# A new order of the steps of four attention layers, given to a list scheduler

## The chip, the cores and the metric

The kernel runs on one core of one Trainium2 chip. The metric is device time in microseconds (us) of one execution, as the median of several runs.

## The reference, cut to what matters

Two blocks follow one another on an input of 256 tokens by 1024 columns, in float32. The first has an attention layer with eight NSA heads and four differential heads ("Even"), an MLP, an attention layer with sixteen MoBA heads ("Odd"), and a second MLP. The second block has two layers of one kind: three branches (a gated delta rule, latent attention and RWKV7) read one projection; their outputs are joined, multiplied by a gate, and projected out.

```python
for i in range(DEPTH):                      # first block, DEPTH = 2
    hn = rms_norm(x, norm_mix[i])
    mix = even_mixer(hn, ...) if i % 2 == 0 else odd_mixer(hn, ...)
    x = x + mix
    x = x + sqrelu_mlp(rms_norm(x, norm_mlp[i]), mlp_w1[i], mlp_w2[i])

# even_mixer: projections, NSA and differential attention, out projection
return jnp.concatenate([o_a, o_b], axis=-1) @ w_out

# second block, gated delta rule: chunks of 64 rows, a state carried along
def step(s, inp):
    w_c, u0_c, p_c, qg_c, kd_c, ge_c = inp
    u = u0_c - jnp.einsum('nhcd,nhde->nhce', w_c, s)
    o = jnp.einsum('nhcd,nhde->nhce', qg_c, s) + jnp.einsum('nhij,nhje->nhie', p_c, u)
    s = ge_c[..., None, None] * s + jnp.einsum('nhcd,nhce->nhde', kd_c, u)
    return s, o
```

RWKV7 is a second recurrence with a carried state, which the kernel also computes in chunks. Both recurrences run forward and backward over the tokens.

## The kernel before, in words

Every layer keeps the 256 tokens as two tiles of 128 rows in SBUF. A weight matrix comes in slabs: `wload` (line 692) issues DMAs into a tile named `wt`, lets ScalarE cast the slab to a rounded copy and VectorE subtract that copy, which leaves a high and a low part in tiles named `fr`. `mm3` (line 719) multiplies each pair as three TensorE products, high by high and the two mixed ones. So in the profile a matmul `ps<-fr 128x256` or `ps<-fr 128x512` is one product of a projection, and a matmul `ps<-sb` belongs to attention, to a transpose or to a recurrence. All other tiles are named `sb` (SBUF) and `ps` (PSUM).

The four attention layers are classes: `Even` (line 1134), `Odd` (1436) and `Second` (1505, used for both layers of the second block). Each consists of parts, and each part is a Python generator that yields after each of its steps:

- Even: `q0`, `q1`, `keys`, `vals`, `gates`, `kc` (projections), `dp0` and `dp1` (projections of two pairs of differential heads), `attn0` to `attn3` (NSA attention), `cmpk` and `comp` (the compressed branch), `diff0` and `diff1` (differential attention), `out_a` and `out_b` (out projection, in two sets of rows of the weight).
- Odd: `proj0` to `proj3`, `attn0` to `attn3`, `out_a`, `out_b`.
- Second: `gdn_proj`, `gdn_prep`, `gdn_inv` (inverses of triangular 64 by 64 matrices, by many small products), `gdn_uw`, `gdn_steps` (the serial recurrence), `gdn_end`; `rwkv_proj`, `rwkv_prep`, `rwkv_inv`, `rwkv_mats`, `rwkv_steps` (the second serial recurrence), `rwkv_end`; `mla_proj`, `mla_attend`, `mla_end`; `gates` (projection and nonlinearity of the output gate), `out_a`, `out_b`.

A string `ORDER` in each class (lines 1140, 1441 and 1576; `Second` has one for each of its layers) says how many steps of which part come next. `Layer.weave` (line 1065) reads it; a word such as `rwkv_inv*4` runs four steps of that part, and the dictionary `NEEDS` says which parts must have ended before a part may begin:

```python
for word in order.split():
    n, _, steps = word.partition("*")
    if n not in parts:
        assert ended >= set(self.NEEDS.get(n, "").split()), (n, ended)
        ...
    for _ in range(int(steps or 1)):
        if self.step(parts[n]):
            ended.add(n)
```

A step does not issue instructions. It notes them (`Order.note`, line 269), and after the last layer `Order.flush` (line 385) hands the whole program to a list scheduler, `Order.plan` (line 412). That walks over the noted operations with a window of 600; on each engine it takes, among the operations whose inputs it believes ready, the one noted first, with a bias for some; it places tiles in SBUF and PSUM as it goes, and does so for several ways of packing, of which one is kept. `put` (line 613, its call is line 614) then issues each operation, so every instruction in the trace carries line 614. Each engine executes its own list in order. The `ORDER` strings thus set priorities, and through them the order of PE (TensorE matmul), DVE (VectorE), ACT (ScalarE), POOL (GpSimd) and SP, whose queue issues the weight loads.

The out projection of a layer has two parts. `out_most` (line 1100), called by `out_a`, multiplies six row slabs of the weight into PSUM; `out_rest` (line 1116), called by `out_b`, multiplies the two others. Their products have 512 columns.

Of the kernel before, what the change touches and what calls it, by code (L numbers as in the profile page):

```python
# [1133 lines left out]
class Even(Layer):  # L1134
# [3 lines left out]
             "attn3": "q1 keys vals gates bias", "diff0": "dp0 lam bias", "diff1": "dp1 lam bias", "cmpk": "kc",  # L1138
             "comp": "cmpk q0 q1 attn0 attn1 attn2 attn3", "out_a": "comp diff0", "out_b": "diff1"}
    ORDER = (  # L1140
# [5 lines left out]

    def run(self):
        net = self.net
# [287 lines left out]
class Odd(Layer):  # L1436
# [2 lines left out]
    NEEDS = {"attn0": "proj0", "attn1": "proj1", "attn2": "proj2", "attn3": "proj3", "out_a": "attn0 attn1 attn2",  # L1439
             "out_b": "attn3"}  # L1440
    ORDER = (
# [4 lines left out]

    def run(self):
        net = self.net
# [56 lines left out]
class Second(Layer):  # L1505
# [41 lines left out]
    def start(self):  # L1547
# [26 lines left out]
        self.ts(self.rh, r, 0.5)  # L1574

    ORDER = (
        "gdn_proj*10 rwkv_proj gdn_proj*4 rwkv_proj gdn_proj*2 rwkv_proj*2 gdn_prep*3 rwkv_proj gdn_prep*3 rwkv_proj "
        "gdn_inv*2 rwkv_proj gdn_inv*2 rwkv_proj gdn_inv rwkv_proj*3 gdn_inv*6 rwkv_proj*2 gdn_inv*2 rwkv_proj "
        "gdn_inv*6 rwkv_proj gdn_inv*2 rwkv_proj gdn_inv rwkv_proj gdn_inv*3 rwkv_proj gdn_inv*5 rwkv_prep gdn_inv*3 "
        "rwkv_prep gdn_inv*6 rwkv_prep*4 gdn_inv gdn_uw rwkv_prep gdn_uw*3 rwkv_prep*2 gdn_uw*2 rwkv_inv*2 gdn_uw "  # L1580
        "rwkv_inv gdn_uw rwkv_inv*4 gdn_uw rwkv_inv gdn_uw rwkv_inv*11 gdn_uw rwkv_inv*2 gdn_steps rwkv_inv gdn_steps "
        "rwkv_inv gdn_steps*2 rwkv_inv*2 gdn_steps rwkv_inv gdn_steps gates gdn_steps*2 rwkv_mats gdn_steps rwkv_inv "
        "rwkv_mats rwkv_inv rwkv_mats rwkv_inv gates rwkv_inv*2 rwkv_mats rwkv_inv*2 rwkv_mats gates*2 rwkv_mats "
        "gdn_steps gates rwkv_mats*2 rwkv_inv gates rwkv_inv gdn_steps rwkv_mats gates rwkv_inv gates rwkv_inv gates "
        "rwkv_mats rwkv_inv rwkv_mats rwkv_steps*2 mla_proj rwkv_steps gates rwkv_steps mla_proj rwkv_steps*2 "
        "mla_proj rwkv_steps mla_proj rwkv_steps*2 gates*2 rwkv_steps mla_proj*3 rwkv_steps mla_proj*2 rwkv_steps "
        "mla_proj gdn_end rwkv_end mla_proj mla_attend*6 rwkv_end mla_attend*6 gdn_end*2 mla_attend*4 rwkv_end*2 "
        "out_b mla_end out_b mla_end out_a out_b out_a*9",
        "gdn_proj*16 gdn_prep*2 gates gdn_prep gates*2 gdn_prep*2 gates gdn_prep gdn_inv gates rwkv_proj gdn_inv*2 "
        "rwkv_proj gdn_inv*3 rwkv_proj gdn_inv*2 rwkv_proj*4 gdn_inv rwkv_proj gdn_inv rwkv_proj gdn_inv*10 "  # L1590
        "rwkv_proj*5 gdn_inv rwkv_proj*3 gdn_inv rwkv_proj gdn_inv*17 rwkv_prep gdn_inv rwkv_prep*4 gdn_uw rwkv_prep "
        "gdn_uw rwkv_prep gdn_uw rwkv_prep gdn_uw rwkv_prep gdn_uw*2 rwkv_inv gdn_uw*3 rwkv_inv*2 gdn_uw*2 gdn_steps "
        "rwkv_inv*2 gdn_steps rwkv_inv*5 gates rwkv_inv*4 gdn_steps rwkv_inv gates rwkv_inv gates rwkv_inv*3 "
        "gdn_steps*3 gates rwkv_inv gdn_steps rwkv_inv gdn_steps gates*3 rwkv_inv rwkv_mats gdn_steps*2 rwkv_mats "
        "rwkv_inv rwkv_mats*3 rwkv_inv rwkv_mats rwkv_inv*8 gdn_steps rwkv_inv rwkv_mats gdn_end mla_proj rwkv_inv "
        "rwkv_mats*3 mla_proj rwkv_inv*4 gdn_end mla_proj rwkv_mats mla_proj*4 rwkv_steps*2 mla_proj rwkv_steps "
        "mla_proj*2 gdn_end rwkv_steps mla_proj rwkv_steps mla_attend*6 rwkv_steps*2 mla_attend*7 rwkv_steps "
        "mla_attend*2 rwkv_steps*2 mla_attend mla_end rwkv_steps mla_end rwkv_steps out_a*2 rwkv_end*2 out_a*3 "
        "rwkv_end out_a*3 rwkv_end out_b*3 out_a*2")

    def run(self):
        net, l = self.net, self.l
# [1012 lines left out]
```

## Time and profile before

| what | us |
|---|---|
| median of 3 runs | 1231.8 (1231.16 to 1233.77) |
| profiled execution, its own time | 1228.06 |
| its span | 1226.3 |
| PE busy | 1073.2 (88%) |
| PEld busy (weight loads of TensorE) | 950.9 (78%) |
| DVE busy | 832.9 (68%) |
| ACT busy | 577.1 (47%) |
| POOL busy | 75.7 (6%) |

The profiled execution is one execution of the program, 3.7 us under the median. The mean granted clock of TensorE over it was 0.905 of 2.4 GHz. The stages follow one another: Even to about 158 us, the first MLP to about 341, Odd to about 461, the second MLP to about 643, the second block's layers to about 928 and 1215, then the final norm and the output. The busy share is an average over these stages, and they have different limits: in the MLPs PE has hardly a gap, while in the second block PE, DVE and ACT take turns in waiting for each other. All idle times are therefore read stage by stage.

### The profile page before, as it was taken

Reading aid. Unit: us, or ns where it says so; the run is one execution under the profiler, and the core shown is the slowest. Engines: PE = TensorE matmul, PEld = TensorE weight load, DVE = VectorE, ACT = ScalarE, POOL = GpSimd, SP = SyncE. Lnnn points to the kernel's source line nnn. Section 1 sums busy time; section 2 is a strip of 40 time slices with the busy share of each in tenths; the row PEclk is TensorE's granted clock in tenths of the full one; section 3 lists DMA queues with packets and bytes.
Section 4 is the critical chain, followed back from the end, with each engine's and each line's share of the span. In section 5 each row is a group of like instructions: output and inputs, shape, how many; then the busy total and the mean of one; then the engine's idle time right before and its main releaser. Section 6 shows DMA issues by size and latency. Waiting matters only on the chain. (4 is left out here: it accounts for less than half of the span.)

```text
span 1226.3 us, 22320 instructions
## 1 busy us (share of the span) xinstructions
PE 1073.2 (88%) x8969; PEld 950.9 (78%) x8969; DVE 832.9 (68%) x1757; ACT 577.1 (47%) x1069; POOL 75.7 (6%) x150
## 2 busy tenths in 40 slices
PE   8999899999998999999997974489899895768895
PEld 7887699999897979999986873478568784657663
DVE  5556775545565566555488899962877889788445
ACT  4565454444436555444354543226564453332751
POOL 0000000000000000000001310002200310001200
PEclk9999899999998999999998885699899797678797
DMA  9930375565542454675671410142214342102110
GB/s 265 275 106 21 118 222 174 177 200 195 174 148 82 143 172 139 222 224 174 210 247 36 132 44 1 51 117 84 70 41 127 86 117 73 36 13 90 51 50 35
DMA packets 129682, 151.51 MB, mean 124 GB/s; under 512 B 15979, under 2 KB 111338, under 8 KB 129578
## 3 DMA queue, kind: packets, MB, share of 16 engines
q1 hardware_dynamic: 128745, 147.89, 38.7%
q0 software_dynamic: 832, 2.20, 0.7%
q8 instruction: 70, 1.15, 0.4%
q14 instruction: 35, 0.28, 0.1%
HBM read 147.42 MB, written 1.07 MB: 121 GB/s over the span
## 5 line engine op out<-in xcount | busy, mean ns | idle before, releaser
L614 PE MATMUL ps<-fr 128*128 128x256 f32 (+3 forms) x5112 | 788.1, 315 | 23.2 <-DVE fr L614 9.2
L614 PEld LDWEIGHTS ps<-fr 128*128 128x128 f32 (+1 forms) x5112 | 714.4, 194 | 83.6 <-DVE fr L614 14.4
L614 PE MATMUL ps<-sb 64*64 64x64 f32 (+14 forms) x3857 | 309.3, 286 | 118.3 <-DVE sb L614 83.3
L614 PEld LDWEIGHTS ps<-sb 64*64 64x64 f32 (+5 forms) x3857 | 241.1, 171 | 179.8 <-DVE sb L614 77.3
L614 DVE TENSOR_TENSOR fr<-wt,fr 128x1024 fp32r<-128x1024 f32 (+4 forms) x269 | 314.7, 1202 | 55.4 <-ACT fr L614 54.8
L614 ACT CAST fr<-wt 128x1024 fp32r<-128x1024 f32 (+4 forms) x269 | 263.0, 1022 | 80.7 <-DMA wt<-in_mlp_w 25.6
L614 ACT ACTIVATE sb<-sb 128x256 f32<-128x256 f32 (+8 forms) x347 | 163.3, 504 | 209.4 <-DVE sb L614 187.2
L614 DVE TENSOR_TENSOR sb<-ps,sb 128x256 f32<-128x256 f32 (+7 forms) x169 | 85.8, 517 | 171.5 <-ACT sb L614 90.0
L614 ACT ACTIVATE sb<-ps 128x384 f32<-128x384 f32 (+7 forms) x166 | 77.3, 475 | 228.2 <-PE ps L614 207.3
L614 DVE TENSOR_TENSOR sb<-sb 128x256 f32<-128x256 f32 (+24 forms) x436 | 146.1, 348 | 10.9 <-POOL sb L614 4.2
L614 DVE SCALAR_TENSOR_TENSOR sb<-sb 128x256 f32<-128x256 f32 (+8 forms) x228 | 88.8, 407 | 20.6 <-ACT sb L614 17.0
L614 DVE TENSOR_TENSOR sb<-sb,ps 128x512 f32<-128x512 f32 (+3 forms) x82 | 46.7, 582 | 31.9 <-PE ps L614 31.5
L614 POOL TENSOR_TENSOR sb<-sb 128x384 f32<-128x384 f32 (+4 forms) x55 | 52.8, 980 | 171.3 <-PE ps L614 97.3
L614 ACT ACTIVATE sb<-ps,sb 128x256 f32<-128x256 f32 (+3 forms) x70 | 34.8, 542 | 47.7 <-PE ps L614 45.7
L614 DVE TENSOR_TENSOR fr<-sb,fr 128x512 fp32r<-128x512 f32 (+1 forms) x38 | 24.7, 649 | 21.5 <-ACT fr L614 21.3
L614 ACT CAST fr<-sb 128x512 fp32r<-128x512 f32 x32 | 19.9, 621 | 32.4 <-DVE sb L614 32.4
L614 DVE COPY sb<-ps 128x384 f32<-128x384 f32 (+9 forms) x45 | 21.3, 478 | 19.7 <-PE ps L614 19.2
L614 POOL MEMSET sb<- 128x2 f32 (+3 forms) x59 | 5.7, 140 | 463.6 <-DVE sb L614 286.8
L614 DVE TENSOR_SCALAR sb<-sb 128x2 f32<-128x2 f32 (+15 forms) x119 | 26.2, 234 | 4.8 <-POOL sb L614 2.0
L614 DVE CUSTOM_DVE_ANT_0 sb<-ps,sb 128x128 f32<-128x128 f32 (+1 forms) x80 | 24.6, 352 | 6.7 <-PE ps L614 3.5
L614 POOL TENSOR_SCALAR sb<-sb 128x2 f32<-128x2 f32 (+1 forms) x8 | 2.5, 312 | 416.9 <-DVE sb L614 416.9
L614 ACT ACTIVATE fr<-ps,sb 128x256 fp32r<-128x256 f32 x52 | 19.8, 488 | 11.5 <-PE ps L614 10.8
(30 smaller groups left out, 162.8 us busy)
## 6 DMA issues: line engine op xcount, KB each, us to landing
wt<-in_mlp_w SPq DMA_DIRECT2D x128, 512.0 KB
wt<-in_w_in SPq DMA_DIRECT2D x38, 512.0 KB
wt<-in_od_w_in SPq DMA_DIRECT2D x24, 512.0 KB
wt<-in_w_out SPq DMA_DIRECT2D x16, 512.0 KB
wt<-in_ev_w_in SPq DMA_DIRECT2D x14, 512.0 KB
wt<-in_ev_w_in SPq DMA_DIRECT2D x16, 256.0 KB
wt<-in_ev_w_out SPq DMA_DIRECT2D x8, 512.0 KB
wt<-in_od_w_out SPq DMA_DIRECT2D x8, 512.0 KB
```

What stands on the lines that cost most here:

```text
L614: fn(*a, **k)
```

## The change

The four `ORDER` strings are replaced: that of Even, that of Odd, and the two of Second. The parts, their steps, the operations in them, `NEEDS`, the scheduler and the tiles are as they were. The strings are tables; two pieces show their form, the end of Even's and the end of that of the last layer:

```diff
@@ Even @@
-        "diff1*2 attn3 diff1 attn1 diff1 cmpk dp0 cmpk attn3 cmpk*2 dp0 cmpk comp dp0 out_b dp0 diff0 comp diff0*4 "
-        "out_b diff0*4 out_b diff0 comp out_a*10")
+        "attn1 diff1 cmpk*2 diff0 cmpk attn3 attn2 attn3 diff1 diff0 comp diff0*6 comp diff0 comp diff0 out_a out_b "
+        "out_a*3 out_b*2 out_a*6")
...
@@ Second, its second layer @@
-        "mla_attend*2 rwkv_steps*2 mla_attend mla_end rwkv_steps mla_end rwkv_steps out_a*2 rwkv_end*2 out_a*3 "
-        "rwkv_end out_a*3 rwkv_end out_b*3 out_a*2")
+        "rwkv_steps*3 mla_attend*2 rwkv_end mla_attend*3 mla_end*2 rwkv_end out_a*3 rwkv_end out_a*3 rwkv_end out_b "
+        "out_a out_b*2 out_a*3")
```

Three places of PE's list follow. A row is a run of equal matmuls; `ps<-fr 128x512` is a product of the out projection.

**End of Even, PE, before.** The `128x128` rows are transposes of the attention outputs, the `128x256` rows multiply their probabilities by values, and the 24 products `128x512` are `out_b`'s.

```order
L614 MATMUL ps<-sb 128x128 x2
L614 MATMUL ps<-sb 128x256 x2
L614 MATMUL ps<-sb 128x128 x9
L614 MATMUL ps<-sb 128x256 x4
L614 MATMUL ps<-sb 128x128 x3
L614 MATMUL ps<-fr 128x512 x24
L614 MATMUL ps<-sb 128x128 x3
L614 MATMUL ps<-fr 128x512 x4
L614 MATMUL ps<-sb 128x128 x3
L614 MATMUL ps<-fr 128x512 x19
L614 MATMUL ps<-sb 128x128 x4
L614 MATMUL ps<-fr 128x512 x49
```

The same place of the changed kernel; three more runs of `128x512` (of 2, 2 and 4) stand ahead of these rows, with one to three `128x128` between them.

```order
L614 MATMUL ps<-sb 128x128 x3
L614 MATMUL ps<-fr 128x512 x2
L614 MATMUL ps<-sb 128x128
L614 MATMUL ps<-fr 128x512 x2
L614 MATMUL ps<-sb 128x128 x2
L614 MATMUL ps<-fr 128x512 x4
L614 MATMUL ps<-sb 128x128 x5
L614 MATMUL ps<-fr 128x512 x5
L614 MATMUL ps<-sb 128x256 x4
L614 MATMUL ps<-fr 128x512 x3
L614 MATMUL ps<-sb 128x128 x4
L614 MATMUL ps<-fr 128x512 x72
```

The 24 products that stood in one piece behind the attention's last small products now stand in eight pieces between them, and the other 72 in one piece at the end.

**First layer of the second block, PE, before.** The `64x64` rows are `gdn_inv`, `gdn_uw` and `gdn_steps`; the `128x320` rows are the first products of `gates`; `32x32` and `128x2` belong to `gdn_inv` and `rwkv_prep`.

```order
L614 MATMUL ps<-sb 128x128 x8
L614 MATMUL ps<-sb 32x32 x96
L614 MATMUL ps<-sb 64x64 x33
L614 MATMUL ps<-sb 128x2 x4
L614 MATMUL ps<-sb 64x64 x239
L614 MATMUL ps<-sb 128x128 x8
L614 MATMUL ps<-fr 128x320 x24
L614 MATMUL ps<-sb 128x128 x8
L614 MATMUL ps<-sb 64x64 x13
L614 MATMUL ps<-fr 128x320 x24
```

The same place of the changed kernel:

```order
L614 MATMUL ps<-fr 128x320
L614 MATMUL ps<-sb 128x128 x7
L614 MATMUL ps<-sb 32x32 x96
L614 MATMUL ps<-fr 128x320 x6
L614 MATMUL ps<-sb 64x64
L614 MATMUL ps<-fr 128x320 x7
L614 MATMUL ps<-sb 128x2 x4
L614 MATMUL ps<-fr 128x320 x2
L614 MATMUL ps<-sb 64x64 x103
L614 MATMUL ps<-fr 128x320 x8
L614 MATMUL ps<-sb 64x64 x144
L614 MATMUL ps<-fr 128x320 x24
```

The first 24 products of `gates`, which stood behind all the `64x64` rows, now stand in five pieces in front of them and between them.

**End of the last layer, PE, before.** The `64x64` and `64x256` rows are the last pieces of `rwkv_steps`, the `128x128` rows transposes, the `128x512` rows products of `out_a`, the last 24 of them of `out_b`. Five more `128x512` stand ahead of these rows.

```order
L614 MATMUL ps<-sb 128x128 x4
L614 MATMUL ps<-fr 128x512
L614 MATMUL ps<-sb 128x128 x4
L614 MATMUL ps<-sb 64x256
L614 MATMUL ps<-sb 64x64 x8
L614 MATMUL ps<-sb 64x256 x3
L614 MATMUL ps<-sb 64x64 x8
L614 MATMUL ps<-fr 128x512 x30
L614 MATMUL ps<-sb 64x64 x16
L614 MATMUL ps<-fr 128x512 x36
L614 MATMUL ps<-sb 128x128 x4
L614 MATMUL ps<-fr 128x512 x24
```

The same place of the changed kernel; three `128x512`, 16 `64x64` and 2 `128x128` stand ahead of these rows, and 38 more products `128x512` behind the last.

```order
L614 MATMUL ps<-fr 128x512
L614 MATMUL ps<-sb 128x128 x2
L614 MATMUL ps<-fr 128x512 x2
L614 MATMUL ps<-sb 64x64 x8
L614 MATMUL ps<-sb 128x128 x4
L614 MATMUL ps<-sb 64x64 x8
L614 MATMUL ps<-sb 64x256 x4
L614 MATMUL ps<-fr 128x512 x51
L614 MATMUL ps<-sb 128x128
L614 MATMUL ps<-fr 128x512
L614 MATMUL ps<-sb 128x128 x3
```

Ahead of the last piece of `rwkv_steps` stood 36 products of the out projection, and now 6; behind it stood 60, and now 90.

## Rows read from the trace of the kernel before

**Rows 1.** The page: busy time, share of the span, instructions; DMA busy tenths in 40 slices.

```profile
PE 1073.2 (88%) x8969; PEld 950.9 (78%) x8969; DVE 832.9 (68%) x1757; ACT 577.1 (47%) x1069; POOL 75.7 (6%) x150
...
DMA  9930375565542454675671410142214342102110
```

**Rows 2.** Windows: length, busy PE, PEld, DVE, ACT, POOL, then clock, DMA share, GB/s.

```profile
51.70:105.70 54.00, 51.80 (x441) 47.42 (x439) 32.35 (x105) 37.63 (x108) 0.00 (x0) 1.00 0.42 124
105.70:158.40 52.70, 44.88 (x240) 34.82 (x240) 36.73 (x84) 22.83 (x49) 3.45 (x5) 0.84 0.31 99
377.10:393.00 15.90, 12.44 (x86) 9.79 (x85) 11.54 (x41) 14.39 (x45) 0.00 (x0) 0.79 0.31 99
737.80:772.00 34.20, 18.30 (x427) 16.83 (x429) 33.34 (x91) 9.74 (x16) 0.52 (x1) 0.50 0.07 17
799.60:850.00 50.40, 44.85 (x514) 41.79 (x508) 25.44 (x41) 21.23 (x35) 4.62 (x7) 0.97 0.37 99
1043.00:1075.80 32.80, 23.75 (x436) 22.00 (x431) 23.61 (x47) 11.36 (x18) 0.52 (x1) 0.66 0.15 33
1075.80:1127.00 51.20, 38.14 (x652) 34.97 (x654) 43.11 (x99) 12.17 (x22) 3.13 (x4) 0.83 0.16 53
1127.00:1184.00 57.00, 50.11 (x470) 35.23 (x465) 29.22 (x85) 40.87 (x97) 11.51 (x16) 0.79 0.19 62
```

**Rows 3.** Timeline of PE, end of the last layer: start, us, operation [idle before <-releaser].

```profile
1183.10 7.12 PE L614 MATMUL ps<-fr 128*128 128x512 f32 x30
1190.14 0.68 PE L614 MATMUL ps<-sb 64*64 64x64 f32 x16
1191.30 1.08 PE L614 MATMUL ps<-sb 128*64 128x64 f32 x16 [0.48 <-ACT sb L614]
...
1194.30 8.37 PE L614 MATMUL ps<-fr 128*128 128x512 f32 x34 [0.34 <-DVE fr L614]
1204.60 0.88 PE L614 MATMUL ps<-sb 128*128 128x128 f32 x4 [1.94 <-DVE sb L614]
1206.17 8.57 PE L614 MATMUL ps<-fr 128*128 128x512 f32 x24 [0.69 <-ACT fr L614]
```

**Rows 4.** Timeline of DVE, the same stretch.

```profile
1186.85 0.69 DVE L614 TENSOR_TENSOR sb<-sb,ps 128x512 f32<-128x512 f32 x1 [2.71 <-PE ps L614]
...
1192.42 0.69 DVE L614 COPY sb<-ps 128x512 f32<-128x512 f32 x1 [1.49 <-PE ps L614]
...
1203.35 1.53 DVE L614 TENSOR_TENSOR sb<-sb 128x512 f32<-128x512 f32 x3
```

**Rows 5.** ACT by shape, 1127 to 1184: count, busy, mean ns, idle before.

```profile
L614 ACT ACTIVATE sb<-ps 64x256 f32<-64x256 f32 x19 | 7.2, 378 | 0.8 <-PE ps L614 0.4
...
L614 ACT ACTIVATE sb<-sb 32x256 f32<-32x256 f32 x12 | 4.6, 409 | 0.2
...
L614 ACT ACTIVATE sb<-sb 64x512 f32<-64x512 f32 x4 | 4.4, 1158 | 8.9 <-PE ps L614 8.9
```

**Rows 6.** Timeline of PE, second block's second layer.

```profile
1060.95 4.64 PE L614 MATMUL ps<-fr 128*128 128x256 f32 x20 [0.20 <-DVE fr L614]
...
1066.23 3.12 PE L614 MATMUL ps<-fr 128*128 128x256 f32 x24
```

**Rows 7.** Timeline of PE, second block's first layer.

```profile
792.02 1.56 PE L614 MATMUL ps<-sb 64*64 64x64 f32 x48 [9.57 <-DVE sb L614]
...
801.66 0.56 PE L614 MATMUL ps<-fr 128*128 128x320 f32 x2
...
806.31 3.59 PE L614 MATMUL ps<-fr 128*128 128x320 f32 x13 [0.65 <-DVE sb L614]
```

**Rows 8.** Timeline of PE, end of Even.

```profile
127.08 1.33 PE L614 MATMUL ps<-sb 128*128 128x128 f32 x5 [3.95 <-DVE sb L614]
...
133.72 5.72 PE L614 MATMUL ps<-fr 128*128 128x512 f32 x24
```

**Rows 9.** Timeline of PE, Odd, first attention.

```profile
383.54 5.37 PE L614 MATMUL ps<-sb 128*128 128x128 f32 x20 [3.43 <-ACT sb L614]
```

More of the change, by code (lines that the diff above doesn't have):

```diff
@@ L1441 @@
     ORDER = (
[4 rows of a table removed]
+        "proj1*6 proj0*6 proj2 proj0*3 proj1 attn0 proj1 proj2 attn0 proj2 proj3*2 proj1 proj2*3 proj3 attn1 proj3*3 "
+        "proj2 attn0*2 attn1*2 attn0*2 proj2*2 attn1*3 attn2*4 proj3*2 attn2 proj3 attn3*3 attn2 attn3 out_a attn3*2 "
+        "out_b*2 out_a*5 out_b out_a*3")
     def run(self):
@@ L1576 @@
     ORDER = (
[L1577 to L1586, printed above, removed]
@@ L1587 @@
-        "mla_proj gdn_end rwkv_end mla_proj mla_attend*6 rwkv_end mla_attend*6 gdn_end*2 mla_attend*4 rwkv_end*2 "
-        "out_b mla_end out_b mla_end out_a out_b out_a*9",
-        "gdn_proj*16 gdn_prep*2 gates gdn_prep gates*2 gdn_prep*2 gates gdn_prep gdn_inv gates rwkv_proj gdn_inv*2 "
-        "rwkv_proj gdn_inv*3 rwkv_proj gdn_inv*2 rwkv_proj*4 gdn_inv rwkv_proj gdn_inv rwkv_proj gdn_inv*10 "
-        "rwkv_proj*5 gdn_inv rwkv_proj*3 gdn_inv rwkv_proj gdn_inv*17 rwkv_prep gdn_inv rwkv_prep*4 gdn_uw rwkv_prep "
@@ L1592 @@
[L1592 to L1596, printed above, removed]
@@ L1597 @@
-        "mla_proj*2 gdn_end rwkv_steps mla_proj rwkv_steps mla_attend*6 rwkv_steps*2 mla_attend*7 rwkv_steps "
-        "mla_attend*2 rwkv_steps*2 mla_attend mla_end rwkv_steps mla_end rwkv_steps out_a*2 rwkv_end*2 out_a*3 "
-        "rwkv_end out_a*3 rwkv_end out_b*3 out_a*2")
+        "gdn_proj*10 rwkv_proj gdn_proj*4 rwkv_proj gdn_proj*2 rwkv_proj gdn_prep rwkv_proj gdn_prep*2 rwkv_proj "
+        "gdn_prep*2 rwkv_proj gdn_prep gdn_inv rwkv_proj*2 gdn_inv rwkv_proj gdn_inv*2 rwkv_proj gdn_inv*2 rwkv_proj "
@@ new lines @@
+        "gdn_inv*3 rwkv_proj gdn_inv*6 rwkv_proj gdn_inv*7 rwkv_proj gdn_inv*5 rwkv_proj*3 gdn_inv*2 rwkv_proj "
+        "gdn_inv rwkv_prep*4 gdn_inv*6 rwkv_prep gdn_inv*2 rwkv_prep gdn_inv*2 rwkv_prep gdn_uw*3 rwkv_prep*2 "
+        "rwkv_inv gdn_uw rwkv_inv*17 gdn_uw*4 rwkv_inv*2 gdn_uw rwkv_inv gdn_uw*2 rwkv_inv gdn_steps*2 rwkv_inv "
+        "gdn_steps rwkv_inv gdn_steps rwkv_inv gdn_steps rwkv_inv gdn_steps gates gdn_steps*2 rwkv_inv rwkv_mats "
+        "gdn_steps gates rwkv_mats rwkv_inv*5 rwkv_mats*2 rwkv_inv gates rwkv_mats*2 gates*2 gdn_steps rwkv_mats*2 "
@@ new lines @@
+        "rwkv_inv gates rwkv_inv gdn_steps rwkv_mats gates rwkv_inv gates rwkv_inv rwkv_mats gates rwkv_inv rwkv_mats "
+        "rwkv_steps mla_proj gates rwkv_steps mla_proj rwkv_steps*2 mla_proj rwkv_steps*2 mla_proj rwkv_steps*2 gates "
+        "rwkv_steps mla_proj rwkv_steps mla_proj*3 rwkv_steps mla_proj*2 gates rwkv_steps gdn_end mla_proj "
+        "mla_attend*2 rwkv_end mla_attend*4 rwkv_end mla_attend*2 rwkv_end mla_attend*4 rwkv_end mla_attend gdn_end*2 "
+        "mla_attend*3 out_b mla_end out_b mla_end out_a*8 out_b out_a*2",
@@ new lines @@
+        "gdn_proj*16 gdn_prep*2 gates gdn_prep gates*2 gdn_prep*2 gates gdn_prep gdn_inv gates rwkv_proj gdn_inv*2 "
+        "rwkv_proj gdn_inv*4 rwkv_proj gdn_inv*3 rwkv_proj gdn_inv*4 rwkv_proj gdn_inv rwkv_proj gdn_inv rwkv_proj*2 "
+        "gdn_inv rwkv_proj gdn_inv rwkv_proj*2 gdn_inv*4 rwkv_proj gdn_inv rwkv_proj*2 gdn_inv*2 rwkv_proj gdn_inv "
+        "rwkv_proj gdn_inv rwkv_proj*2 gdn_inv*7 rwkv_prep gdn_inv rwkv_prep gdn_inv rwkv_prep*2 gdn_inv*4 "
+        "rwkv_prep*5 gdn_uw*6 rwkv_inv gdn_uw*2 rwkv_inv*2 gdn_uw rwkv_inv*2 gdn_uw rwkv_inv*8 gdn_uw gdn_steps gates "
@@ new lines @@
+        "rwkv_inv*3 gdn_steps rwkv_inv*4 gdn_steps gates gdn_steps*2 gates rwkv_inv gates gdn_steps*3 gates rwkv_inv "
+        "gates rwkv_inv rwkv_mats gdn_steps*2 rwkv_inv rwkv_mats*4 gates rwkv_inv*2 gdn_steps rwkv_inv*6 rwkv_mats "
+        "gdn_end rwkv_mats mla_proj rwkv_inv rwkv_mats*3 rwkv_inv mla_proj rwkv_inv*2 gdn_end rwkv_inv mla_proj*6 "
+        "rwkv_mats mla_proj rwkv_inv mla_proj*2 rwkv_steps*2 mla_attend rwkv_steps mla_attend rwkv_steps mla_attend*2 "
+        "rwkv_steps*2 mla_attend*3 rwkv_steps mla_attend rwkv_steps mla_attend*2 gdn_end rwkv_steps mla_attend "
```

10 rows, old and new, of the table ORDER are left out of this document.

## The prediction

> **What bounds the kernel now.** I began with the page. PE is busy for 88% of the span, DVE for 68%, ACT for 47% [rows 1]. No engine is full, so no single busy time gives the answer: the layers must be read stage by stage. The windows came next [rows 2]; there the reader is to see three kinds of stretch. In 51.7–105.7 (Even) PE is busy 51.80 of 54.0 us at clock 1.00: PE bounds it. In 737.8–772.0 DVE is busy 33.34 of 34.2 us and PE 18.30: VectorE bounds it. In 105.7–158.4, 377.1–393.0 and 1043.0–1075.8 no engine is full: PE is busy 44.88 of 52.7, 12.44 of 15.9 and 23.75 of 32.8 us, at a clock of 0.84, 0.79 and 0.66. There a chain of small pieces over PE, DVE and ACT sets the time, and an order that lays independent products into its waits can gain. The timelines then show which products stand ahead of a chain, and which behind it.
>
> No operation changes, so each term is a wait filled or opened. The sum is made against the profiled execution, 1228.06 us, which is 3.7 us below the median of 1231.8; at the end I add the 3.7.
>
> **1. End of the last layer: −6 us.** Before, a run of 30 products of 512 columns, 7.12 us from 1183.10, stands directly ahead of the last piece of `rwkv_steps`, whose 16 products follow at 1190.14 with no wait [rows 3]: their inputs were there, PE held them back. VectorE in turn waits 2.71 us for PE at 1186.85 and copies the last result at 1192.42 [rows 4]. Now those 30 stand behind the steps, so the steps can end 7.12 us earlier, at 1192.38 − 7.1 = 1185.3. Then 90 products follow; at 7.12/30 = 0.237 us each they take 21.4, and four transposes 0.9 [rows 3]: PE ends at 1207.6 instead of 1206.17 + 8.57 = 1214.74, which is −7.1. Late next would be `rwkv_end` on VectorE: from the copy at 1192.42 to 1203.35 + 1.53 it takes 12.5 us [rows 4], and the first 51 of the 90 products, 12.1 us, cover it. ScalarE takes some back: its list now has six more copies 64x256 and six more 32x256 ahead of the first `rwkv_steps` copies, 6 × 0.378 + 6 × 0.409 = 4.7 us, while the two weight casts moved up as well fall into its 8.9 us of waiting [rows 5]. Later in the chain that lead shrinks, so I take 1 us off. Ends: −10, if the waits of 1.94 and 0.69 us at 1204.60 and 1206.17 go too; +7, if the chain's end does not move and the 30 products simply follow it.
>
> **2. Second block's second layer, 44 products of `gates`: −2.** They stand at 1060.95 and 1066.23, 4.64 + 3.12 = 7.76 us [rows 6], ahead of the products that lead into `gdn_steps`. Now they stand behind the second of its steps, directly ahead of the third. What is taken from the chain's front is put into its middle: at 0.13 us each (3.12/24) they cost 5.7 there. The difference is 2. Ends: −7.8, if in the new place they fall into waits (PE is busy only 38.14 of 51.2 us in 1075.8–1127 [rows 2]); +6, if the old place was a wait anyway and the new one is not.
>
> **3. Second block's first layer, 24 products of `gates`: −4.** They run from 801.66 to 806.31 + 3.59 = 809.90, 8.24 us, partly waiting for DVE [rows 7], behind the chain of `gdn_steps`, in a stretch where PE is busy 44.85 of 50.4 us [rows 2]. Now they stand between the products of `gdn_inv` and `gdn_uw`, in 737.8–799.6, where PE waits for DVE, up to 9.57 us at a time [rows 7]. They cost nothing there as long as DVE sets the time; if that cover fails they cost up to their 8.24 us again, and nothing is won. The other 24 now stand ahead of the ninth step of the chain. I take half of 8.24. Ends: −8.2 and +4, the latter if the chain gets later by those other 24 (24 × 0.13 = 3.1) and one wait.
>
> By the Trainium skill ("TensorE: Matmul & The Clock Gate", Terms) the price of throttled time is that time multiplied by 1 − K/N, the share of pulses withheld. By it the 34.2 us at clock 0.50 would hold 17 us to be won. The rows speak against it: PE is busy for 18.30 of those 34.2 us, and DVE for 33.34 [rows 2], so a faster PE would wait for DVE. In the sum this counts as nothing; it is a rival below.
>
> **4. End of Even: −5.** PE waits 3.95 us at 127.08, and `out_b`'s 24 products come only afterwards, 5.72 us in one piece at 133.72 [rows 8]. Now they stand in eight pieces between the small products. In the window PE is idle for 52.7 − 44.88 = 7.8 us [rows 2]; 5 of the 5.72 us should fit. Ends: 0, if the pieces stand one step too late for each wait; −9, if the clock of 0.84 also recovers.
>
> **5. Middle of Even: +3.** The five product groups of `dp0`, 144 products, now come after the softmax pieces instead of between them. At 0.13 us they take 18.7 of PE's 51.80 us in 51.7–105.7, which leaves 33.1 for PE to do beside ScalarE's 37.63 [rows 2]. ScalarE is longer by 4.5 and becomes the bound of this stretch. I take 3, as some exponentials may come after `dp0`. Ends: 0 and +5. This is the only place where I expect a loss.
>
> **6. Odd: −5.** PE waits 3.43 us for ACT at 383.54 and then runs 20 transposes in 5.37 us [rows 9]; the window loses 15.9 − 12.44 = 3.5 us in waits and has a clock of 0.79 [rows 2], worth up to 15.9 × 0.21 = 3.3 more. Now three projections come first and 72 products stand behind six softmax pieces; 72 × 0.13 = 9.4 us more than fill the wait. Ends: 0 and −6.5.
>
> Costed at nothing: `keys` ahead of `vals`, and the moved weight loads on SP's queue. The loads are covered by the products of the slab before; DMA is full only in the first two of the 40 slices [rows 1], where slabs of one size change places. If that cover went, PE would wait one load at the start of a part. POOL's few moved instructions (3.45 us in 105.7–158.4, 0.52 in 1043–1075.8 [rows 2]) lie beside idle time. The MLPs and the final norm are not touched.
>
> **Sum:** −6 − 2 − 4 − 5 + 3 − 5 = −19. 1228.06 − 19 = 1209.1, plus 3.7 for the median: 1213 us. All lower ends together give −41.5 (1190), all upper ends +22 (1254).
>
> **The rivals.** (a) *VectorE sets both layers of the second block, and the waits at Even's end are not filled.* Then terms 2, 3 and 4 are 0, and −6 + 3 − 5 = −8 gives 1224. For it: the 33.34 of 34.2 us of DVE; against it: in 1043–1075.8 DVE is busy only 23.61 of 32.8 us [rows 2].
>
> (b) *The clock comes back.* The products laid into 737.8–772.0 keep PE busier there, its clock rises from the half level, and the small products get shorter; 1213 − 17 = 1196. This is the page's rule taken at its word (the skill's section above). Against it stands DVE at 33.34 us.
>
> (c) *Nothing comes of it.* The strings only set priorities; PE, at 88%, has 153 us of idle time in all, and what is filled in one place opens in another: 1232. Against it: PE's list differs at all three places shown above, and terms 1 and 6 start from waits that one can see.
>
> (d) *Slower: the serial chains set the second block's time, and their cover has been moved away.* The place is the end of the last layer, and the point that decides is whether the 16 products at 1190.14 come earlier at all. If `rwkv_steps` is late because of ScalarE (40.87 of 57.0 us busy in 1127–1184 [rows 2], with 4.7 us of copies more ahead of it) and not because of the 30 products, its end stays at 1192.38, and 90 products follow it instead of 60: +7 in place of −6. The same mechanism gives the upper ends of terms 2 and 3, +6 and +4. With terms 4 to 6 as forecast: +7 + 6 + 4 − 5 + 3 − 5 = +10, 1242. For it: `rwkv_steps` passes its results through ScalarE copies. Against it: the row at 1190.14 has no wait.
>
> **How the numbers follow.** The forecast, 1213, gets 0.53, with a range of its own of 1201 to 1225 (some 12 us either side, from the ends of its larger terms taken at random). (a) gets 0.18, (b) 0.04, (c) 0.10, (d) 0.15. About 0.2%, 2.5 us, is what a measurement of this kernel can tell from no change. Faster: 0.53 + 0.18 + 0.04 = 0.75; the same: 0.10; slower: 0.15. The range runs from 1197, which leaves out half of (b) and the low tail of the forecast, to 1240, which leaves out rather more than half of (d): about 0.15 together.
>
> **What would show it.** In the changed profile: the last `rwkv_steps` products about 7 us before the time at which the old order had them (counted from the layer's start), and then one run of some 90 products `128x512` without a wait over 1 us (term 1); no wait of 3.4 us before Odd's first transposes (term 6); waits under 1 us between Even's `128x512` pieces (term 4); waits of PE for ACT in Even's middle, about 3 us in all (term 5); no run of `128x320` directly behind `gdn_steps` (term 3). The prediction is wrong if the last piece of `rwkv_steps` starts after a wait for ACT or DVE of several us, if DVE in 737.8–799.6 gets longer, or if Even's middle loses over 5 us.

## The result and the profile after

The changed kernel runs in 1202.35 us (median of 4 runs, 1200.65 to 1206.77), against 1231.48 for the kernel before in the same comparison. The ratio is 0.9766, with a 95% interval of 0.9734 to 0.9799. The forecast was 1213 us, 19 us less than before; the measured difference is 29 us. The profiled execution took 1200.65 us (before: 1228.06), so its parts can be set against the terms of the sum.

The page of the changed kernel, the lines that answer to [rows 1]:

```profile
PE 1062.2 (89%) x8969; PEld 944.8 (79%) x8969; DVE 833.8 (70%) x1757; ACT 575.6 (48%) x1069; POOL 73.4 (6%) x150
...
DMA  8933266556553456556671410132304233203110
```

VectorE, ScalarE and GpSimd did the same work in nearly the same time; only PE's busy time fell, by 11 us, since more of its products ran at the full clock (the mean granted clock is 0.914, and was 0.905). The rest of the 27 us is waiting of PE that has gone.

Every instruction of the trace can be given to its step by its place in its engine's list. Read that way, the layers end at these times (us from the start of the span):

| end of | before | changed | difference | gained or lost in the layer | forecast for it |
|---|---|---|---|---|---|
| Even | 159.1 | 149.5 | -9.6 | -9.6 | -2 (terms 4, 5) |
| first MLP, Odd, second MLP | 642.6 | 626.7 | -16.0 | -6.4 | -5 (term 6) |
| second block, first layer | 928.1 | 916.5 | -11.6 | +4.4 | -4 (term 3) |
| final norm | 1220.8 | 1193.8 | -27.0 | -15.4 | -8 (terms 1, 2) |

So the sum was too small by 8 us, and one layer went the other way from its forecast. The windows of the changed kernel answer to [rows 2]: Even's middle, Even's end in two pieces, then three of the second block.

```profile
52.00:98.00 46.00, 44.45 (x395) 40.74 (x392) 31.11 (x112) 39.16 (x116) 0.00 (x0) 1.00 0.48 151
...
111.00:125.00 14.00, 13.29 (x87) 10.50 (x88) 8.61 (x40) 7.46 (x25) 0.68 (x1) 0.76 0.11 41
125.00:149.50 24.50, 22.73 (x109) 18.20 (x107) 19.58 (x25) 11.72 (x17) 1.20 (x2) 1.00 0.33 108
```

```profile
722.00:758.00 36.00, 16.30 (x370) 14.38 (x371) 32.34 (x87) 8.22 (x13) 0.53 (x1) 0.57 0.11 28
758.00:790.00 32.00, 15.35 (x370) 13.75 (x366) 28.27 (x68) 9.10 (x14) 0.00 (x0) 0.69 0.11 31
790.00:838.00 48.00, 41.21 (x514) 37.91 (x514) 24.65 (x40) 20.11 (x32) 5.19 (x8) 0.93 0.35 90
```

In Even's middle PE is busy for 44.45 of 46.0 us although ScalarE is now busy for 39.16 of them: ScalarE did not become the bound. At Even's end PE has 0.7 and 1.8 us of idle time in the two pieces, where it had 7.8 us before. In the second block's first layer VectorE still fills 32.34 of 36.0 us.

PE's timeline at the end of Even, the place of [rows 8]:

```profile
118.10 1.22 PE L614 MATMUL ps<-fr 128*128 128x512 f32 x2
...
130.99 0.66 PE L614 MATMUL ps<-sb 128*128 128x128 f32 x4 [1.46 <-DVE sb L614]
131.40 16.81 PE L614 MATMUL ps<-fr 128*128 128x512 f32 x72
```

The wait of 3.95 us is gone; the one left is 1.46 us. In Odd, at the place of [rows 9], 72 products now run up to the first transposes, which no longer wait:

```profile
386.25 9.24 PE L614 MATMUL ps<-fr 128*128 128x256 f32 x72
395.33 3.23 PE L614 MATMUL ps<-sb 128*128 128x128 f32 x28
```

And the end of the last layer, where [rows 3] stood:

```profile
1161.17 1.06 PE L614 MATMUL ps<-sb 64*64 64x64 f32 x34
...
1163.08 3.26 PE L614 MATMUL ps<-sb 64*64 64x64 f32 x44
1166.27 11.89 PE L614 MATMUL ps<-fr 128*128 128x512 f32 x51
1178.04 0.33 PE L614 MATMUL ps<-sb 128*128 128x128 f32 x1
...
1178.69 8.98 PE L614 MATMUL ps<-fr 128*128 128x512 f32 x38
```

The 90 products run without a wait and at the full clock (8.98 / 38 = 0.236 us each), as term 1 had them; the last 24 before took 8.57 us. On VectorE the copy that begins `rwkv_end`, at 1192.42 in [rows 4], comes at 1165.41, and on ScalarE the two weight casts that were moved up fall into the wait of [rows 5], which is still 8.54 us long behind them:

```profile
1165.41 0.69 DVE L614 COPY sb<-ps 128x512 f32<-128x512 f32 x1 [2.00 <-PE ps L614]
```

```profile
1113.20 1.99 ACT L614 CAST fr<-wt 128x1024 fp32r<-128x1024 f32 x2
1123.73 4.47 ACT L614 ACTIVATE sb<-sb 64x512 f32<-64x512 f32 x4 [8.54 <-PE ps L614]
```

### The profile page after: what moved, and what is told of

The parts are those of the page before. It is cut to its first block, busy times and chain, and to the rows that moved or that the text cites. A ratio compares the mean times of both kernels' runs of the same rounds, so it can differ in the third digit from the quotient of the medians.

```text
span 1198.9 us, 22350 instructions
## 1 busy us (share of the span) xinstructions
PE 1062.2 (89%) x8969; PEld 944.8 (79%) x8969; DVE 833.8 (70%) x1757; ACT 575.6 (48%) x1069; POOL 73.4 (6%) x150
## 5 line engine op out<-in xcount | busy, mean ns | idle before, releaser
L614 PE MATMUL ps<-sb 64*64 64x64 f32 (+12 forms) x3857 | 297.3, 277 | 105.5 <-DVE sb L614 77.3
L614 PEld LDWEIGHTS ps<-sb 64*64 64x64 f32 (+4 forms) x3857 | 233.5, 163 | 163.1 <-DVE sb L614 76.0
L614 DVE TENSOR_TENSOR sb<-sb 128x256 f32<-128x256 f32 (+26 forms) x436 | 147.2, 352 | 11.9 <-PE ps L614 2.8
L614 DVE SCALAR_TENSOR_TENSOR sb<-sb 128x256 f32<-128x256 f32 (+9 forms) x228 | 90.1, 413 | 16.4 <-ACT sb L614 12.9
L614 POOL TENSOR_TENSOR sb<-sb 128x384 f32<-128x384 f32 (+4 forms) x55 | 51.6, 958 | 137.2 <-PE ps L614 77.9
L614 DVE TENSOR_SCALAR sb<-sb 128x256 f32<-128x256 f32 (+15 forms) x119 | 25.6, 230 | 5.0 <-POOL sb L614 2.0
```

The costliest lines, as they stand in the source:

```text
L614: fn(*a, **k)
```

## The experiments

**One string at a time.** Four kernels came first. Three have a single new string among the old ones, the fourth has three new strings and the old one in the second block's first layer.

Even alone (the other strings as before):

```diff
 class Even(Layer):
...
-        "gates q0 vals q0 lam q0 gates vals keys q1 keys*2 bias kc q1 vals q0 dp1 bias keys gates attn0 kc attn0 kc "
+        "gates q0 keys gates vals gates vals q0 vals q1 keys q0 bias*2 q0 keys dp1 kc keys attn0 dp1 lam*2 attn0 dp1 "
...
```

> Only Even has the new order. Theory (the four orders act each in its own layer, and their differences add): the changed profile has Even's end 9.6 us earlier than before, so this kernel is 9.6 us below the kernel before, about 1222. Rival (part of the gain at Even's end belongs to what Odd's new order pulls forward): less than 6 us, over 1226.

Measured: 1215.96 us (1211.44 to 1216.95), ratio 0.9871, interval 0.9823 to 0.9919, some 15 us faster. Even ends 12.9 us earlier than before, 3.3 more than in the changed kernel; 4 more us came, in the trace, in layers whose strings had not been touched; single traces of one list differ by as much (last section).

The second block's first layer alone:

```diff
 class Second(Layer):
...
-        "gdn_proj*10 rwkv_proj gdn_proj*4 rwkv_proj gdn_proj*2 rwkv_proj*2 gdn_prep*3 rwkv_proj gdn_prep*3 rwkv_proj "
+        "gdn_proj*10 rwkv_proj gdn_proj*4 rwkv_proj gdn_proj*2 rwkv_proj gdn_prep rwkv_proj gdn_prep*2 rwkv_proj "
...
```

> Only the second block's first layer has the new order. In the changed profile that layer loses 4.4 us against the kernel before. Theory (its own order costs this): 4.4 us slower, about 1236. Rival (my term 3: the order gains 4 us, and the loss comes from how the list scheduler joins this layer to the changed layers around it): about 1227.5.

Measured: 1213.91 us (1213.2 to 1218.5), ratio 0.986, interval 0.9816 to 0.9904. Neither expectation held: 17 us faster. But in the layer that was changed the trace shows a gain of only 1 us; 12 us were gained in the last layer, whose string is the old one.

The last layer alone:

```diff
 class Second(Layer):
...
-        "rwkv_proj gdn_inv*3 rwkv_proj gdn_inv*2 rwkv_proj*4 gdn_inv rwkv_proj gdn_inv rwkv_proj gdn_inv*10 "
+        "rwkv_proj gdn_inv*4 rwkv_proj gdn_inv*3 rwkv_proj gdn_inv*4 rwkv_proj gdn_inv rwkv_proj gdn_inv rwkv_proj*2 "
...
```

> Only the last layer has the new order. Theory (each order acts in its own layer): 15.4 us faster, about 1216, of which some 11 us come between the end of the latent attention and the end of the RWKV steps. Rival (a part of it came from the layer before ending in another state, with casts for the last layer done earlier): 11 us or less, 1220 or more.

Measured: 1235.96 us (1229.8 to 1238.36), ratio 1.0027, interval 1.0005 to 1.0049: slower, if anything. Its tail gained 11.7 us between the end of the latent attention and the final norm, as in the changed kernel, but 13 us were lost ahead of that inside the layer.

The changed kernel without its new string in the second block's first layer (that string back as before, the other three new):

```diff
 class Second(Layer):
...
-        "gdn_proj*10 rwkv_proj gdn_proj*4 rwkv_proj gdn_proj*2 rwkv_proj gdn_prep rwkv_proj gdn_prep*2 rwkv_proj "
+        "gdn_proj*10 rwkv_proj gdn_proj*4 rwkv_proj gdn_proj*2 rwkv_proj*2 gdn_prep*3 rwkv_proj gdn_prep*3 rwkv_proj "
...
```

> The changed kernel with the old order in the second block's first layer. Theory (that layer's new order costs 4.4 us by itself): 4.4 us under the changed kernel's 1202.4, about 1198. Rival (the loss comes with the joints to the other layers): 1202 to 1207.

Measured: 1222.57 us (1216.68 to 1225.95), ratio 0.9927, interval 0.9902 to 0.9953. Not the 1198 that the theory gave: 20 us slower than the changed kernel. The layer with the old string took 307.9 us in its surroundings (end of the second MLP at 624.5, end of the layer at 932.4), where the same string had given 285.5 before.

The theory that each string acts in its own layer fell. The lists show why it had to: the scheduler walks over the whole program, and with one string changed it also issued other layers differently. With the second block's first layer changed, 64 of 1595 PE entries and 70 of 539 VectorE entries of the *last* layer change places; with that layer's string put back in the changed kernel, 281 of its own PE entries stand elsewhere than in the kernel before. A string is not an order.

**Written lists.** In the next kernels the scheduler does not choose what comes next; each engine's list is written out as a table, and it only places the tiles.

```diff
+        script = {e: l[::-1] for e, l in lists().items()}
         while p < n:
             best = None
-            for e in self.ENGINES:
-                c, seen = None, 0
...
+            for e in self.ENGINES:
+                i = script[e][-1] if script[e] else None
+                if i is None or need[i] or i > p + window:
+                    continue
+                s = start(i, e)
...
```

The last layer's lists from the changed kernel, all others from the kernel before:

> Here the scheduler no longer chooses: each engine's list is written out, that of the kernel before everywhere, and in the last layer that of the changed kernel. Theory (a layer's time follows from the issued lists, and the earlier runs differed because a changed string also changes the lists of layers whose string is unchanged): the last layer is 15.4 us shorter, as in the changed profile, about 1215.5. Rival (that layer's gain depends on the state the layer before leaves, such as TensorE's clock): less than 8 us, over 1223.

Measured: 1229.35 us (1222.02 to 1236.79), ratio 0.9971, interval 0.9947 to 0.9995.

The first layer's lists of the second block from the changed kernel, all others from before:

> The lists of the kernel before, written out, and in the second block's first layer those of the changed kernel. Theory (the issued lists decide, and this layer's new lists cost 4.4 us): about 1235. Rival (the loss of 4.4 us in the changed profile came from its surroundings, as the run with this string alone, at 1213.9, suggests): 1231 or less.

Measured: 1255.17 us (1250.05 to 1256.6), ratio 1.0175, interval 1.0144 to 1.0205: 24 us slower, a miss for both sides.

In both, layers with exactly the lists of before ran longer than before: in the first of them the second block's first layer took 294.2 us instead of 285.5, in the second of them the last layer took 16 us longer. What differed there was the places of the tiles, which the scheduler had chosen anew, and the granted clock (in the first, 0.79 over that layer where it was 0.83); the two were not separated, and of the first one's 9 us some 5 may lie between single traces anyway. For the 16 us of the second that is too little: lists alone do not fix the time either. VectorE's timeline in the first of these two, in a layer whose lists are those of before, shows one such wait, for a piece of SBUF that products of another step still read:

```profile
847.96 2.29 DVE L695 TENSOR_TENSOR sb<-sb,ps 64x384 f32<-64x384 f32 x4 [6.85 <-PE ps L695]
```

That this wait is one for a place stands in the tables of places and in the waits of the program that is built from them; what it costs was not tried by itself.

**Term 1 alone.** Written lists of before, with 30 products moved on PE and four additions on VectorE. Here all but 12 of the 2064 tiles kept their places. On PE:

```diff
-out_a: MATMUL ps<-fr 128x512 x30
 rwkv_steps: MATMUL ps<-sb 64x64 x16
+out_a: MATMUL ps<-fr 128x512 x30
 out_a: MATMUL ps<-fr 128x512 x36
```

> Term 1 alone: the written lists of the kernel before, with the 30 products of 512 columns that stood ahead of the last piece of the RWKV steps moved behind it on PE, and four additions of the out projection moved behind the chain of rwkv_end on VectorE. Theory (PE held the steps back, as term 1 says): the steps end 7.1 us earlier and the kernel is 7.1 us faster, about 1224. Rival (d) (the chain's end does not move): 7 us slower, about 1238.

Measured: 1227.67 us (1224.55 to 1230.26), ratio 0.9962, interval 0.9943 to 0.9982, which is 2 to 7 us faster. PE's timeline:

```profile
1187.45 0.68 PE L695 MATMUL ps<-sb 64*64 64x64 f32 x16 [0.54 <-DVE sb L695]
1188.61 1.08 PE L695 MATMUL ps<-sb 128*64 128x64 f32 x16 [0.48 <-ACT sb L695]
1189.62 15.43 PE L695 MATMUL ps<-fr 128*128 128x512 f32 x66
1204.89 0.60 PE L695 MATMUL ps<-sb 128*128 128x128 f32 x4
1206.18 6.01 PE L695 MATMUL ps<-fr 128*128 128x512 f32 x24 [0.69 <-ACT fr L695]
```

The steps end at 1188.61 + 1.08 = 1189.7 against 1192.4 before. In this execution everything had been 5.4 us late at the end of the layer before, with the same lists; TensorE had run part of that layer's products at the half clock (last section). Against the end of its own latent attention the steps came 6.4 us earlier, and the final norm 6.2. So the mechanism of term 1 holds alone, with some 6 us in the trace and 2 to 7 by the medians; rival (d) is out.

**Term 3 alone.** Written lists of before, with 24 products of the gate moved on PE into the long wait:

```diff
 gdn_steps, step 4: MATMUL ps<-sb 64x64
+gates: MATMUL ps<-fr 128x320 x24
 gdn_steps, step 6: MATMUL ps<-sb 64x64
...
-gates: MATMUL ps<-fr 128x320 x24
```

> Term 3 by itself: the written lists of the kernel before, with the 24 products of the gate that stood behind gdn_steps moved on PE into the 9.57 us wait ahead of its sixth step. Theory (that wait belongs to VectorE, so they are free there): 8.2 us faster, about 1223. Rival (a) (VectorE sets the stretch behind them as well, so taking them out wins nothing): within 2 us of the kernel before.

Measured: 1249.85 us (1247.31 to 1251.05), ratio 1.0136, interval 1.0112 to 1.0161: 19 us slower. PE's timeline:

```profile
785.19 2.19 PE L695 MATMUL ps<-sb 64*64 64x64 f32 x48 [1.90 <-DVE sb L695]
799.21 5.75 PE L695 MATMUL ps<-fr 128*128 128x320 f32 x24 [11.84 <-DVE sb L695]
804.89 0.93 PE L695 MATMUL ps<-sb 64*64 64x64 f32 x48
```

The products did not go into the wait; they stood in it themselves, for 11.84 us, and the chain behind them. The inputs of the first of them were ready at 772 and the last of their weights at 778, and their PSUM bank, bank 4, was free from 782. But the wait ended with the VectorE instruction that read a tile of `gdn_steps` in the banks 1 and 7. It was not the only wait of this kind: the scheduler had placed the tiles anew, 975 of them in SBUF and 166 in PSUM. Of some 18 us that the trace is longer than before, 10.3 were lost in the layer with the moved products and 7.7 in the last layer, whose lists are unchanged. There the 24 products of the gate, in bank 2, stand behind a VectorE instruction that reads the banks 0 and 5, where before they ran without a wait:

```profile
1105.58 5.42 PE L695 MATMUL ps<-fr 128*128 128x256 f32 x24 [8.65 <-DVE sb L695]
```

The same pattern is in the changed kernel. ScalarE there, in the last layer:

```profile
1061.48 0.49 ACT L614 ACTIVATE sb<-ps 128x384 f32<-128x384 f32 x1 [0.22 <-PE ps L614]
1067.37 0.49 ACT L614 ACTIVATE sb<-ps 128x384 f32<-128x384 f32 x1 [5.40 <-PE ps L614]
```

The second instruction copies a tile of `gdn_steps` in the banks 1 and 7. PE had finished it before those products began, and yet ScalarE waited until PE had run all 48 products of the gate, whose tiles lie in the banks 5 and 6. A tile of two banks is addressed as two pieces with a step between them, and the suspicion is that the program's waits are made for the whole stretch from the first bank to the last. Summed over the trace, waits that nothing else explains and that end with an instruction in a bank in between come to 16 us in the kernel before (11 of them on PE) and to 27 in the changed one (13 on PE, 7 on VectorE, 7 on ScalarE).

The longest of this kind in the changed kernel is not in the 27. In the first layer of the second block ScalarE copies a tile of `rwkv_mats` in bank 4, and stands 17.58 us until VectorE has read a tile of `gdn_steps` in the banks 2 and 5:

```profile
766.41 0.87 ACT L614 ACTIVATE sb<-ps 128x384 f32<-128x384 f32 x2 [0.22 <-PE ps L614]
784.86 0.60 ACT L614 ACTIVATE sb<-ps 128x512 f32<-128x512 f32 x1 [17.58 <-DVE sb L614]
```

With it, and one more of 3 us on ScalarE, the sum is some 49 us. The engines wait side by side, so such a sum is not what the waits cost.

**Only the PSUM banks.** The last four kernels have every engine's list and every place written out:

```diff
-        preds = self.graph()
-        best, fail = None, None
...
-        self.expected, self.log, self.at, self.starts = best
+        self.log, self.at = np.cumsum(unpack(LIST)).tolist(), places()
```

In the first two the lists and all places in SBUF are those of the changed kernel and of the kernel before, and only PSUM banks differ.

> The changed kernel with every engine's list and every SBUF place kept; only the PSUM banks of 367 of its 474 PSUM tiles are other ones. Theory (an instruction that touches a tile in two banks also waits for, and holds up, the banks between the two; in the changed profile such waits add up to 27 us, some 13 of them on PE): with banks chosen so that none lies between the two of a tile in use, 8 to 15 us faster than the changed kernel, 1187 to 1194. Rival (those waits are covered by others): within 3 us of 1202.

Measured: 1181.29 us (1179.27 to 1182.74), ratio to the kernel before 0.9588, interval 0.9562 to 0.9615: 21 us less than the changed kernel, more than the theory gave.

> The kernel before with every list and every SBUF place kept and other PSUM banks. Theory (the same waits; in its profile they add up to 16 us, 11 of them on PE): 5 to 9 us faster than before, 1222 to 1226, so that the change's gain is the same with either choice of banks. Rival (the kernel before has no such wait on its path): within 2 us of 1231.

Measured: 1220.16 us (1218.38 to 1221.8), ratio 0.9906, interval 0.9881 to 0.993: 11 us less than the kernel before by the ratio (0.0094 x 1231.5 = 11.6), again more than the theory gave. In both, the waits of that kind are down to some 2 us in the whole trace. The place where ScalarE had waited 5.40 us, with the new banks (1 and 4 for the tile, 6 and 7 for the products):

```profile
1045.44 0.87 ACT L726 ACTIVATE sb<-ps 128x384 f32<-128x384 f32 x2 [0.22 <-PE ps L726]
```

Both copies now run in one go. The place of the 17.58 us, in the changed kernel with new banks, keeps a wait of 0.22 us, and the layer is 10.0 us shorter:

```profile
766.35 1.36 ACT L726 ACTIVATE sb<-ps 128x384 f32<-128x384 f32 x3 [0.22 <-PE ps L726]
```

So the suspicion is borne out. The Trainium skill ("PSUM — Partial Sum Buffer", "PSUM bank collisions raise a hardware error") says that two engines collide in one and the same quadrant of partitions of one bank, while the same accesses to different banks run clean. The two runs agree: the copy at 1045.44, of the banks 1 and 4, ran beside products in the banks 6 and 7, which go from 1045.28 to 1051.3. The waits can also be read in the programs that are built. In the changed kernel the copy at 1067.37 waits for PE's count behind the last of the 48 products, in bank 5, though the count already stood behind the tile's own products one step earlier. The moved products wait in the same way for the read of the banks 1 and 7, and the three waits among the gate's products in [rows 7] are of products in bank 2 for reads of tiles in the banks 0 and 4, and 1 and 7. Waits for one and the same bank to come free did not get fewer with the new banks: on PE they went from some 11 to some 23 us in the changed kernel. So it is the program that asks for these waits. The waits themselves were not rewritten.

The changed kernel with new banks is the fastest of all that were run, 4.1% under the kernel before. And the change, with neither side hampered by its banks, is worth 1220.2 - 1181.3 = 39 us. By the layers of the two traces: Even 11.3, Odd with the MLPs 5.5, the second block's first layer 2.0, the last layer 19.3.

**Terms 3 and 2 with free banks.** The lists of before, the 24 products moved as in the run that lost 19 us, other banks:

> Term 3 again, as the run before it with the same 24 products of the gate moved into the 9.57 us wait on PE, but with banks chosen so that the products' bank does not lie between the two of a tile in use. Theory (the 19 us that this move cost came from one bank): 3 to 8 us faster than the kernel before with new banks alone, some 1217 to 1221. Rival (the products themselves disturb the chain): 1235 or more.

Measured: 1221.21 us (1219.37 to 1224.13), ratio 0.9913, interval 0.9887 to 0.9939. The 19 us are gone, and with them the waits for banks in between: they come to 37 us in the slower run and to some 3 in this one. The places in SBUF went back to those of before in the same step, so what they had cost is not told apart. But it is not faster than the 1220.16 without the move. The two timelines, first without and then with the move:

```profile
794.08 1.56 PE L727 MATMUL ps<-sb 64*64 64x64 f32 x48 [9.84 <-DVE sb L727]
...
803.60 3.79 PE L727 MATMUL ps<-fr 128*128 128x320 f32 x24
807.31 2.01 PE L727 MATMUL ps<-sb 64*128 64x128 f32 x42
```

```profile
783.99 5.11 PE L727 MATMUL ps<-fr 128*128 128x320 f32 x24
794.26 1.56 PE L727 MATMUL ps<-sb 64*64 64x64 f32 x48 [5.16 <-DVE sb L727]
...
805.61 2.00 PE L727 MATMUL ps<-sb 64*128 64x128 f32 x40 [1.32 <-DVE sb L727]
```

The products lie in the wait, which costs the chain nothing (794.26 after 794.08), and behind the chain 1.7 us are won, not 8.2: in the old place, with free banks, the 24 products take 3.79 us instead of the 8.24 of [rows 7], and 1.32 of them covered another wait. The layer ends 2.4 us earlier, and that is lost again in the next one.

The 48 products of the last layer behind the second of the `gdn_steps`, the lists of before otherwise, new banks:

> Term 2 by itself: the lists of the kernel before with the 48 products of the gate in the last layer moved on PE behind the second of the gdn_steps, with banks chosen as in the run before. Theory (term 2: what leaves the chain's front enters its middle, full clock for half clock): 2 us faster than the kernel before with new banks alone. Rival (the upper end of term 2: the old place was a wait anyway): 4 to 6 us slower than that.

Measured: 1221.69 us (1216.65 to 1223.34), ratio 0.9911, interval 0.9886 to 0.9937; not told apart from 1220.16. In the trace the layer is some 1.5 us longer than without the move. A gain of 2 us is not shown, nor the loss of 4 to 6.

## Why the prediction was right, and where its terms were off

The forecast's direction, its likeliest case and its range held; the size did not: 19 us forecast, 29 measured. Step by step:

- **Term 1** (end of the last layer, -6): right in its mechanism. Alone it gave some 6 us by the trace, 2 to 7 by the medians. In the changed kernel the stretch from the end of the latent attention on is 11.2 us shorter. Beside the 7.1 the waits of 1.94 and 0.69 us went, which was the lower end of the term. The last 24 products also ran at the full clock: at 0.236 us each they take 5.7 us where they took 8.57, and these 2.9 us stood in no term. ScalarE's copies came 5.6 us later against their surroundings, as priced, but the chain caught up, so the deduction of 1 us was not needed.
- **Term 2** (-2): alone nothing that can be told from 0. The front of the last layer gained 4.2 us in the changed kernel; what else in its lists brought that was not taken apart.
- **Term 3** (-4): the sign was wrong in the changed kernel, where the layer lost 4.4 us. The failing step is the sentence that the 24 products cost nothing "as long as DVE sets the time". VectorE does set it, but in the new lists it has more to do ahead of the chain. From the end of the second MLP to the first product of `gdn_steps` it is busy for 127.70 us instead of 120.91, and the stretch takes 137.2 us instead of 129.7. The windows, before and then changed:

```profile
642.60:772.30 129.70, 96.04 (x1006) 88.19 (x1008) 120.91 (x324) 57.04 (x108) 17.44 (x28) 0.76 0.20 58
626.70:763.90 137.20, 100.39 (x1052) 90.64 (x1054) 127.70 (x326) 58.38 (x110) 18.99 (x28) 0.79 0.21 61
```

That VectorE gets longer there was one of the prediction's signs of being wrong. With the new banks the new lists also lengthen the stretch, from 131.7 to 136.7 us, so the banks explain at most part of it; VectorE's longer work as its cause was not tried by itself. Behind it the term's upper end came: the other 24 products stand in the chain, and the ninth step follows the eighth after 6.3 us where it followed after 1.4.

```profile
788.52 4.61 PE L614 MATMUL ps<-fr 128*128 128x320 f32 x24 [0.19 <-DVE sb L614]
```

The step also looked at engines and not at what else an early product holds: its PSUM bank, and with it the tiles that reach across that bank. With other banks the layer is 10.0 us shorter in the changed kernel and 3.7 in the kernel before, and then its new lists gain 2.0 us. And it took the 8.24 us of [rows 7] as the price of the products, while more than half of it was such waits and time at a lower clock; with free banks they take 3.79.

- **Term 4** (-5) **and term 5** (+3): together -9.6 instead of -2. Over the whole layer PE's idle time fell from 15.45 to 10.3 us, as term 4 had priced it, and its busy time from 143.65 to 139.20, which is the returning clock that the term's lower end allowed for. Of its signs one did not come: a wait of 1.46 us is left. Term 5 was wrong: it took all 144 products of `dp0` out of the stretch and set ScalarE's 37.63 us against the 33.1 that PE had left. In the changed kernel 57 of the 144 are still in 52 to 98, with 12 of `kc` and small products of the attention beside those of `dp1`. PE is busy for 44.45 of 46.0 us, ScalarE for 39.16, and no PE wait there reaches 0.8 us.
- **Term 6** (-5): -6.4. The wait of 3.43 us went as described.
- **Rival (a)** was right that VectorE sets the stretch in the first layer of the second block, though term 3 came to +4.4 there and not to 0, and wrong about the rest. **Rival (b)**, the returning clock: in 722–758 VectorE is busy for 32.34 of 36.0 us and PE's clock is 0.57, where it was 0.50; the 17 us did not come. **Rival (c)** is out by the interval, **(d)** by the run of term 1.
- **What the prediction did not see** is the kind of wait that cost 11 us in the kernel before and 21 in the changed one. It was in the rows: at the place of [rows 7] the gate's products wait three times for VectorE without any input coming from there, at 806.31 and at the two places ahead of it. The prediction had counted this as part of the products' price.

```profile
803.02 0.85 PE L614 MATMUL ps<-fr 128*128 128x320 f32 x4 [0.80 <-DVE sb L614]
804.65 1.00 PE L614 MATMUL ps<-fr 128*128 128x320 f32 x5 [0.79 <-DVE sb L614]
```

That the sum came no further off is in part luck: by the table the layer of term 3 came out 8 us worse than forecast and the others together 16 us better, so the errors partly cancel.

What stays open: where in the last layer the further 4 us came from, whether VectorE's longer work in the first layer is what its 7 us are, and how much of the 8 to 16 us by which layers with unchanged lists differed is due to places in SBUF, how much to PSUM banks and how much to the clock.

## What to carry to other kernels

An order given to a scheduler is judged by the lists and the places that come out, over the whole program: the same string gave a layer of 285 and one of 308 us here, so a part of such a change is tested by fixing the lists and the places, not by putting back one string. Before a product is laid into a wait, ask what it holds while it is there (a PSUM bank, a place in SBUF), and who else touches that. A wait that ends with an instruction which delivers nothing to the waiting one was here a wait for a place, or for a bank that only lay between the two banks of a tile; choosing other PSUM banks, with no operation or list changed, was worth 21 us in the changed kernel and 11 us in the kernel before, beside the 29 us of the whole new order.

## What the runs showed of the hardware that was not expected

TensorE's clock is not a function of the lists: in the run of term 1 the second block's first layer had the lists of before and, but for 12 tiles of the whole program, its places; its 24 products of the gate ran from 802.41 to 812.5, where they had taken 8.24 us [rows 7]. The granted clock over 796 to 813 was 0.50, the half level, while before it was 0.77 over 796 to 810. The layer ended 5.4 us later than in the trace of before. A difference of that size between two single traces is not to be read as the effect of a change; the medians of several runs, or the same stretch against its own surroundings, are the better measure.
